# Backbone layer: when the weight sums of the fifth product are requested, who forms one sum, and who copies one head's output

## The chip, the cores and the metric

The kernel runs on one core of one Trainium2 chip. The metric is the device time of one execution in microseconds (us); lower is better. The kernel before was timed in 3 runs: median 903.42 us, from 902.72 to 903.51. One more execution was taken with the hardware profiler. It took 907.04 us, and all rows below come from it. Its span, from the first instruction to the last, is 905.3 us.

TensorE (PE) multiplies, VectorE (DVE) and ScalarE (ACT) do elementwise work, GpSimd (POOL) and SyncE (SP) mostly issue DMA transfers. Every transfer runs on the core's 16 DMA engines, whichever queue it was issued from. In the profile q0 is POOL's queue, q1 is SP's and q10 is ScalarE's.

## The reference

One layer of a diffusion backbone over 512 latent tokens and 256 context tokens, width 1024, all in float32. The part that matters here is the token mixer:

```python
z = h @ w_in
u, vs, q, r, ga, gb, k, v, lr = _split(z, IN_SPLITS)
a = _spatial_gating(gelu(u), gelu(vs), ...)
o, s_f, s_b = _gla_bidir(qh, k, v, lr, ...)          # 4 heads, chunked linear attention
o = o * lax.rsqrt(jnp.mean(o * o, axis=-1, keepdims=True) + EPS)
ob = (o * gla_norm_g) * jax.nn.silu(r)
merged = sigmoid(ga) * (a @ w_br_a) + sigmoid(gb) * (ob @ w_br_b)
return merged @ w_o
```

A modulated norm stands before it, and a convolutional feed-forward block with two more large products (`ffn_w_up`, `ffn_w_down`) behind it.

## The kernel before

**Arithmetic.** Every float32 operand of a product is split into a rounded high part and a remainder, and each product takes three matmuls (high by high, high by low, low by high). A weight tile goes from DRAM into a tile `raw` (SP issues it, L240), ScalarE rounds it to `wh` (the cast of L255), VectorE forms `wl = raw - wh` (L256), and PE uses the pair. `raw` has 5 buffers (`RAW`), `wh` and `wl` 5 each.

**Order of the work.** The weight tiles stand in one list, `specs`. A call of `weights()` takes the next pair; on the way it splits up to two tiles further (`stream_split`) and requests loads up to four tiles further (`stream_load`). Positions 0 to 17 serve the heads' q, k and v and then the eight column blocks of u (`u0` to `u7`, positions 10 to 17); `R_AT` is 18. Then come five large products of 14 positions each: r (18 to 31), vs (32 to 45), ga (46 to 59), gb (60 to 73) and the product with `w_br_a`, called br_a here (74 to 87). `w_br_b`, `w_o` and the feed-forward weights follow. In time r starts at 246.16 us, vs2 at 300.84, ga3 at 352.72 and gb at 378.1.

**The five products.** Each is done as a 2 by 2 block product with seven block products instead of eight (`gate`). Block product m of r is called r0 to r6, and so on; each takes two positions (two halves of the contraction) and 24 matmuls. Results lie in three pairs of PSUM banks, X, Z and Y, and go out by ScalarE copies (`taken`, L1341) or VectorE operations; bank pair X serves block products 0, 2, 4 and 6. The seven weight operands are three plain quarters of the weights and four sums of quarters.

**The sums.** Sums of quarters are formed in DRAM by transfers that POOL issues (`sums_build`): a plain copy of a quarter into a buffer `sum` (L221), then transfers that add a second quarter or another sum onto it (L223). Each carries 512 KB. A product needs 8 such requests per half, 16 in all. For the first three products (`g < ADDED`, r, vs and ga) the first sum is formed on the core instead: the positions of block product 1 load the second quarter raw, VectorE adds the raw tile of two positions earlier onto it (L251) before the cast, and 6 requests per half remain, 12 in all. The raw tile of two positions earlier keeps its buffer until that addition.

**When the sums are requested.** `gate_sums` walks through the requests of r, vs, ga, gb and br_a in this order, 68 in all. `weights()` takes the next one or two of them at each position below `R_AT`, and above it at those that `gate_pace` names; `hook()`, which is called between pieces of other work (twice in each u block), takes one more. `behind_pe` makes each request wait for the last matmul written before it.

```python
def gate_pace(i):
    return i % 3 if i > 45 else i % 4 == 0
...
def hook():
    hooked[0] += 1
    if (hooked[0] % 2 or pos[2] >= 8) and pos[2] < R_AT:
        next(building[1][1], None)
```

Followed by hand, this gives 42 requests before u0, 22 in u0 to u7 (10 of gb, of which 2 plain, and 12 of br_a, of which 8 plain), and one each at r1, r3, r5 and vs0.

**Other transfers around it.** In u, SP also reads back pieces of the normed input (`fq<-fx`) for the sums of activations. In r to ga it reads columns of `w_ada` (`wa`), and ScalarE's queue writes intermediate results to DRAM (`kept`). At the start of gb, SP reads `a` back in 16 pieces (`aq<-kept`, L1501).

**Head outputs.** `step_o` forms four output tiles of a head in PSUM; VectorE copies each to SBUF (L1020), and ScalarE then squares and sums the same tile (L1022). Only after both is the bank free. The four heads run between the other products; the second head (`h == 1`) ends at about 172 us.

Of the kernel before, what the change touches and what calls it, by code (L numbers as in the profile page):

```python
# [38 lines left out]
SHSC = 6  # L39
WT = (1, 1)  # L40
RAW = 5
ADDED = 3


@with_exitstack
def backbone_kernel(
# [7 lines left out]
    V, A, G, T = nc.vector, nc.scalar, nc.gpsimd, nc.tensor  # L54
# [19 lines left out]
    def late(shape, dt=F32, s="l"):  # L74
        return lp.tile(shape, dt, tag="l", name=nm(s))
# [7 lines left out]
    def gl():  # L83
        return pg.tile([P, 512], F32, tag="gl", name=nm("gl"))
# [81 lines left out]
    R_AT = len(specs)  # L166
# [14 lines left out]
    def w_block(ap, kn=2, back=0):  # L181
        specs.append((ap.rearrange("(k p) c -> p k c", p=P), kn, 512, back))
# [9 lines left out]
    for g, (g_quarter, g_sums) in enumerate(gate_weights):  # L192
        for n, f in enumerate((lambda b: g_quarter(b, 0, 0),
                               lambda b: g_quarter(b, 0, 1) if g < ADDED else g_sums[b][0], lambda b: g_sums[b][1],
                               lambda b: g_quarter(b, 1, 0), lambda b: g_sums[b][3], lambda b: g_quarter(b, 1, 1),
                               lambda b: g_sums[b][2])):
            for b in range(2):
                w_block(f(b), back=2 if n == 1 and g < ADDED else 0)
    down_specs[R_AT:R_AT] = specs
# [13 lines left out]
    def sums_build(quarter, sums, added=False):  # L213
        for step in ((((1, (0, 0)), (2, (1, 0)), (3, (0, 1))), ((3, (1, 1)),), ((1, 3),), ((2, 1),)) if added else
                     (((0, (0, 1)), (1, (1, 1)), (2, (1, 0)), (3, (0, 1))), ((0, (0, 0)), (3, (1, 1))),
                      ((1, 0),), ((2, 1),))):
            for b in range(len(sums)):
                for dst, src in step:
                    ap = quarter(b, *src) if isinstance(src, tuple) else sums[b][src]
                    if len(step) > 2:  # L220
                        behind_pe(lambda: G.dma_start(sums[b][dst], ap), G)  # L221
                    else:
                        behind_pe(lambda: G.dma_start(sums[b][dst], ap, accum_op=ALU.add), G)  # L223
                    yield

    def gate_sums():
        for g, z in enumerate(gate_weights):
            yield from sums_build(*z, g < ADDED)

# [3 lines left out]
    pos = [0, 0, 0]  # L233
# [37 lines left out]
        return lambda: V.tensor_tensor(wl, raw, wh.bitcast(F32), op=ALU.subtract)  # L271

    def gate_pace(i):
        return i % 3 if i > 45 else i % 4 == 0

    def weights():
        i = pos[2]
        pos[2] += 1
        for at, steps_ in building:
            for _ in range((i >= at and (at > 1 or i < R_AT or gate_pace(i))) + (at <= i < DENSE)):  # L280
                next(steps_, None)
        stream_split(i + 2)
        stream_load(i + 1 + AHEAD)
        return splits.pop(i)
# [648 lines left out]
    def mm3(ps, a, b, start, stop):  # L933
        for z, (p_, q_) in enumerate(((a[0], b[0]), (a[0], b[1]), (a[1], b[0]))):
            T.matmul(ps, p_, q_, start=(start and z == 0), stop=(stop and z == 2))  # L935
# [75 lines left out]
    def step_o(h, part):  # L1011
        S_ = heads[h]
        for i in ((1, 2), (0, 3))[part]:
            po = gl()
            oc = po[:, :256]
            for d in range(2):
                mm3(oc, [z[:, i * P:(i + 1) * P] for z in S_["qs"][d]], S_["st"][d][i], d == 0, False)
            mm3(oc, [z[:, i * P:(i + 1) * P] for z in S_["pt"]], S_["v"][i],
                False, True)
            V.tensor_copy(S_["o"][i // 2][:, i % 2, :], oc)  # L1020
            junk = late([P, 256], BF16, s="junk")
            A.activation(junk, oc, AF.Square, accum_out=oss[:, h, i:i + 1])  # L1022
        if part == 1:
            S_.clear()
# [3 lines left out]
    hooked = [0]  # L1028

    def hook():  # L1030
        hooked[0] += 1
        if (hooked[0] % 2 or pos[2] >= 8) and pos[2] < R_AT:
            next(building[1][1], None)
        if hooks:
            f = hooks.pop(0)
            f[0](*f[1:])
# [4 lines left out]
    def ctx_k(h, part):  # L1041
        ps = mm()
        for k in range(KT):
            wh, wl = part(k)
            ah, al = hc[k]
            for i, (a, b) in enumerate(((wh, ah), (wh, al), (wl, ah))):
                T.matmul(ps[:, :LC], a, b, start=(k == 0 and i == 0), stop=(k == KT - 1 and i == 2))  # L1047
        kcs[h] = heap([P, LC], s="kc")
        A.copy(kcs[h], ps[:, :LC])
        hook()  # L1050
# [5 lines left out]
    def x_unit(store, h):  # L1056
        w = weights()
        ps = mm()
        prod_cm(ps, w, hx)
        store[h] = heap([P, S], s="kq")  # L1060
        if store is qxs:
            A.mul(store[h], ps, QS)
        else:
            V.tensor_copy(store[h], ps)
        hook()
        return lambda k: [z[:, k, :] for z in w]

    def v_units():

        ws = [weights() for _ in range(KT // 2)]  # L1070
        v = []
        for t in range(6):
            ps = mm()
            for k in range(KT):
                wide_step(ps, ws[k // 2], hx if t < 4 else hc, t % 4, k)
            v.append(split_act(ps, s="v", lo_pool=late if t < 3 else heap, hi_pool=late, eng=A.copy))
            for h in (2, 3):
                heads[h].setdefault("v", []).append([z[:, (h - 2) * 256:(h - 1) * 256] for z in v[t]])
            hook()
            hook()  # L1080

    def steps(h):
        if h + 1 < NH:
            rest = [(step_u, h, 0, 3), (step_z, h + 1), (lambda: None,)]
        else:
            rest = [(step_u, h, n, n + 1) for n in range(3)]
        return [(step_transpose, h), (step_scores, h), (step_s0, h)] + rest + [(step_o, h, 0), (step_o, h, 1)]
# [854 lines left out]
```

## Time and profile before

| what | value |
|---|---|
| median of the timed runs | 903.42 us (902.72 to 903.51) |
| profiled execution | 907.04 us |
| its span | 905.3 us |
| PE busy | 888.0 us (98%) |
| VectorE busy | 733.9 us (81%) |
| ScalarE busy | 481.4 us (53%) |
| q0 (POOL): moved, share of 16 engines | 61.04 MB, 31.0% |
| q1 (SP): moved, share of 16 engines | 140.53 MB, 48.6% |
| mean granted TensorE clock | 0.996 of full |

A share of the DMA engines is the time that packets took, over 16 engines and the stretch in question. Packets overlap a little, so a full stretch shows up to about 1.1. The groups of the profile name a line, an engine, an operation and tiles as output<-input; "idle before" is the time that the engine waited just before the instruction, with what released it. The time to landing of a transfer runs from its issue to its completion.

### The profile page before, as it was taken

To read this page: it belongs to the slowest core of one execution; us is meant where nothing else is said; L and a number is where in the kernel's file an instruction comes from. 1 tells how busy PE (TensorE), PEld (TensorE's weight loads), DVE (VectorE), ACT (ScalarE), POOL (GpSimd) and SP (SyncE) were. 2 spreads that over 40 slices of the span, in tenths; PEclk is the share of its full clock that TensorE was granted. 3 is DMA by queue.
4 is the path that set the end of the run, shared out by engine and by line. 5 is a ranking of instruction groups with operands and counts; after the bars stand their busy time and mean duration, and the time that the engine had idled before them with its cause. 6 is when DMAs were issued, how large, how long until landed. Compare 5 with 4: busy or idle time off the path is not lost.

```text
span 905.3 us, 12519 instructions
## 1 busy us (share of the span) xinstructions
PE 888.0 (98%) x4440; PEld 739.6 (82%) x4440; DVE 733.9 (81%) x1223; ACT 481.4 (53%) x795; POOL 96.6 (11%) x150
## 2 busy tenths in 40 slices
PE   7999999999999999999999999999999999999996
PEld 5778888888877888888888889888888888888885
DVE  6478687969739889769998658897899987896996
ACT  6356465757636765577432348433343334356663
POOL 1302222222200000000000010001111110000000
PEclk9999999999999999999999999999999999999999
DMA  9976999999999977778995961998998893356552
GB/s 298 360 242 171 247 280 212 195 289 247 315 269 280 342 243 259 261 240 274 368 364 165 292 179 47 280 303 180 189 219 178 176 193 98 92 167 207 173 180 99
DMA packets 160268, 207.66 MB, mean 229 GB/s; under 512 B 9625, under 2 KB 88805, under 8 KB 160205
## 3 DMA queue, kind: packets, MB, share of 16 engines
q1 hardware_dynamic: 132861, 140.53, 48.6%
q0 software_dynamic: 24352, 61.04, 31.0%
q10 hardware_dynamic: 2992, 5.28, 1.5%
q8 instruction: 35, 0.57, 0.2%
q14 instruction: 28, 0.23, 0.1%
HBM read 198.43 MB, written 67.11 MB: 293 GB/s over the span
## 4 chain that ended last, share of the span: by engine, by line
PE 90%; DMA 4%; DVE 2%; ACT 2%; issue 0%; SPq 0%; ACTq 0%
PE mm L399 32%; PE mm L1358 13%; PE mm L417 10%; PE gl L1839 10%; PE gl L1358 5%; PE gl L935 2%; PE mm L699 2%; DMA fq<-fx 2%; DMA raw<-in_w_in_dram 2%; PE mm L1839 2%; PE gl L699 1%; PE mm L1047 1%; PE mm L1097 1%; PE gl L417 1%; PE gl L608 1%; PE gl L970 1%
## 5 line engine op out<-in xcount | busy, mean ns | idle before, releaser
L255 ACT CAST wh<-raw 128x1024 fp32r<-128x1024 f32 x189 | 194.8, 1036 | 189.3 <-PE mm L399 89.0
L256 DVE TENSOR_TENSOR wl<-raw,wh 128x1024 fp32r<-128x1024 f32 x189 | 226.1, 1203 | 61.8 <-ACT wh L255 60.2
L399 PE MATMUL mm<-h2h,wh 128*128 128x512 f32 (+1 forms) x344 | 133.0, 387 | 0.0
L399 PE MATMUL mm<-h2l,wh 128*128 128x512 f32 (+1 forms) x344 | 133.0, 387 | 0.0
L399 PE MATMUL mm<-h2h,wl 128*128 128x512 f32 (+1 forms) x344 | 133.0, 387 | 0.0
L1691 DVE SCALAR_TENSOR_TENSOR cacc<-ca,ccol,cacc 128x441 f32<-128x441 f32 (+2 forms) x176 | 121.9, 695 | 4.4
L399 PEld LDWEIGHTS mm<-h2h,wh 128*128 128x128 f32 x344 | 64.6, 188 | 13.1
L399 PEld LDWEIGHTS mm<-h2h,wl 128*128 128x128 f32 x344 | 64.6, 188 | 13.1
L399 PEld LDWEIGHTS mm<-h2l,wh 128*128 128x128 f32 x344 | 64.6, 188 | 13.0
L1839 PE MATMUL gl<-wh,dah 128*128 128x512 f32 x132 | 51.3, 389 | 0.0
L1839 PE MATMUL gl<-wl,dah 128*128 128x512 f32 x132 | 51.3, 389 | 0.0
L1839 PE MATMUL gl<-wh,dal 128*128 128x512 f32 x132 | 51.3, 389 | 0.0
L221 POOL DMA_DIRECT2D sum<-in_ffn_w_down_dram x24 | 13.2, 554 | 310.2 <-PE mm L417 196.1
L1188 DVE SCALAR_TENSOR_TENSOR acc<-wa,cs,acc 128x512 f32<-128x512 f32 x64 | 46.3, 749 | 0.0
L1692 ACT ACTIVATE cacc<-cacc 128x512 f32<-128x512 f32 x22 | 13.9, 633 | 59.4 <-DVE cacc L1691 59.4
L1358 PE MATMUL mm<-wh,xs 128*128 128x512 f32 x128 | 42.4, 402 | 2.7 <-ACT dt L1341 2.7
L223 POOL DMA_DIRECT2D sum<-sum x32 | 27.8, 869 | 149.0 <-PE mm L399 54.9
L399 PE MATMUL mm<-hxh,wh 128*128 128x512 f32 x104 | 40.9, 393 | 0.0
L399 PE MATMUL mm<-hxl,wh 128*128 128x512 f32 x104 | 40.6, 391 | 0.0
L399 PE MATMUL mm<-hxh,wl 128*128 128x512 f32 x104 | 40.5, 390 | 0.0
L1358 PE MATMUL mm<-wh,hxh 128*128 128x512 f32 x96 | 37.7, 393 | 0.0
L1358 PE MATMUL mm<-wh,hxl 128*128 128x512 f32 x96 | 37.4, 390 | 0.0
(473 smaller groups left out, 2018.0 us busy)
## 6 DMA issues: line engine op xcount, KB each, us to landing
raw<-sum SPq DMA_DIRECT2D x54, 512.0 KB, 4.9
raw<-in_w_in_dram SPq DMA_DIRECT2D x50, 512.0 KB, 9.2
wa<-in_w_ada_dram SPq DMA_DIRECT2D x96, 256.0 KB, 5.3
raw<-in_ffn_w_up_dram SPq DMA_DIRECT2D x44, 512.0 KB, 5.9
sum<-in_w_in_dram POOLq DMA_DIRECT2D x36, 512.0 KB, 8.8
sum<-sum POOLq DMA_DIRECT2D x30, 512.0 KB, 7.9
sum<-in_ffn_w_down_dram POOLq DMA_DIRECT2D x30, 512.0 KB, 7.2
raw<-in_ffn_w_down_dram SPq DMA_DIRECT2D x15, 512.0 KB, 3.7
```

What stands on the lines that cost most here:

```text
L223: behind_pe(lambda: G.dma_start(sums[b][dst], ap, accum_op=ALU.add), G)
L255: A.copy(wh, raw)
L256: V.tensor_tensor(wl, raw, wh.bitcast(F32), op=ALU.subtract)
L399: T.matmul(ps, a[:, k, :], b[:, c0:c0 + n], start=(k == 0 and i == 0), stop=(k == KT - 1 and i == 2))
L417: T.matmul(ps, a[:, t * P:(t + 1) * P], b[:, k % 2, :], start=(k == 0 and i == 0), stop=(k == KT - 1 and i == 2))
L699: T.matmul(fps[i], a, b, start=(k == 0 and z == 0), stop=(k == KT - 1 and z == 2))
L935: T.matmul(ps, p_, q_, start=(start and z == 0), stop=(stop and z == 2))
L1188: behind_last(lambda: V.scalar_tensor_tensor(acc[i], coming.pop(0), cs[:, k, 0:1], acc[i], op0=ALU.mult, op1=ALU.add), V)
L1358: T.matmul(banks[t], a(kk, t), w[:, kk, :], start=(first and b == 0 and kk == 0 and i == 0), stop=(b == 1 and kk == 1 and i == 2), skip_gr ...
L1691: V.scalar_tensor_tensor(o, a_[:, r0 + dy:r1 + dy, c0 + dx:c1 + dx], wcol(tap), o, op0=ALU.mult, op1=ALU.add)
L1692: A.activation(acc, acc, AF.Gelu)
L1839: T.matmul(ps, a, w[:, kk, :], start=(first and kk == 0 and i == 0), stop=(last and kk == n_ - 1 and i == 2), skip_group_check=True)
```

## The change

Three edits. First, gb joins the products whose first sum VectorE forms from two raw tiles (`ADDED` 4): gb has 12 requests instead of 16, in all 64 instead of 68, and VectorE has two more additions of 128x1024. Second, `hook()` takes no request once position 10 has been passed, so that in u only the eight `weights()` calls take one each; and `gate_pace` takes one at every fourth position in r and at every second from vs on. Followed by hand, u now has the last 6 requests of gb (all additions, u0 to u5) and 2 of br_a (u6, u7); r0, r2, r4 and r6 have one each, vs0 to vs6 one each, ga0 to ga2 one each. Of br_a's 16, the eight plain copies come from u6 to vs1, and the eight additions from vs2 to ga2. Third, the four output copies of the second head go from VectorE to ScalarE.

```diff
-ADDED = 3
+ADDED = 4
...
     def gate_pace(i):
-        return i % 3 if i > 45 else i % 4 == 0
+        return (i - R_AT) % (4 if i < R_AT + 14 else 2) == 1
...
-            V.tensor_copy(S_["o"][i // 2][:, i % 2, :], oc)
+            (A.copy if h == 1 else V.tensor_copy)(S_["o"][i // 2][:, i % 2, :], oc)
...
     def hook():
         hooked[0] += 1
-        if (hooked[0] % 2 or pos[2] >= 8) and pos[2] < R_AT:
+        if (hooked[0] % 2 or pos[2] >= 8) and pos[2] <= R_AT - 8:
             next(building[1][1], None)
```

## The prediction

> **What bounds the kernel now.** I read the head of the page first, then PE's waits, then the place of the longest wait that lies inside the work, engine by engine.
>
> ```profile
> span 905.3 us, 12519 instructions
> PE 888.0 (98%) x4440; PEld 739.6 (82%) x4440; DVE 733.9 (81%) x1223; ACT 481.4 (53%) x795; POOL 96.6 (11%) x150
> ...
> PE mm L463 <- DMA rows<-in_b_ada_dram: 5.5, 1, 5.5
> PE mm L1358 <- ACT dt L1341: 2.7, 1, 2.7
> ...
> 270.41 0.39 PE L1358 MATMUL mm<-wh,xs 128*128 128x512 f32 x1
> 273.53 0.80 PE L1358 MATMUL mm<-wh,xs 128*128 128x512 f32 x1 [2.73 <-ACT dt L1341]
> ...
> 276.54 0.39 PE L1358 MATMUL mm<-wl,xs 128*128 128x512 f32 x1
> ...
> 277.86 5.46 PE gl L1358 x24
> ...
> 270.00:275.00 5.00, 2.27 (x8) 1.52 (x7) 2.17 (x5) 3.06 (x7) 0.00 (x0) 0.80 0.89 315
> ```
>
> PE is the bound: 905.3 - 888.0 leaves 17.3 us, most of it at the two ends (5.5 us is the first load). No edit removes a matmul, so only a gap in PE's row can be won. In the middle there is one of size: in r4, 2.73 us, waiting for a bank that ScalarE had not copied out. It costs more than it shows. From 273.53 to 276.54 PE started 7 matmuls in 3.01 us; at the undisturbed pitch (5.46 / 24 = 0.2275) they need 1.59. The granted clock, column eight of the last row, is 0.80 of full over those 5 us. So 1.42 us went to the slow clock, and the gap is worth 2.73 + 1.42 = 4.15 us.
>
> The Trainium skill, "TensorE: Matmul & The Clock Gate", section "What's actually happening", has the clock halved after an idle window of about 3.4 us, by which a gap of 2.73 us could pass unpunished and removing it would be worth 2.73; the row with 0.80 shows the loss here, and I go by the row.
>
> Why was ScalarE late?
>
> ```profile
> 262.95 1.05 ACT L255 CAST wh<-raw 128x1024 fp32r<-128x1024 f32 x1 [5.12 <-DMA raw<-sum]
> 263.91 0.58 ACT L1341 COPY dt<-mm 128x512 f32<-128x512 f32 x1
> 266.69 1.05 ACT L255 CAST wh<-raw 128x1024 fp32r<-128x1024 f32 x1 [2.20 <-DMA raw<-sum]
> 271.94 1.04 ACT L255 CAST wh<-raw 128x1024 fp32r<-128x1024 f32 x1 [4.21 <-DMA raw<-in_w_in_dram]
> 272.89 0.58 ACT L1341 COPY dt<-mm 128x512 f32<-128x512 f32 x1
> ...
> 239.18 17.21 DMA fq<-fx
> 256.45 15.39 DMA raw<-in_w_in_dram
> ...
> q0 software_dynamic: 1064, 2.11, 76.0%
> q1 hardware_dynamic: 1067, 1.47, 33.0%
> ...
> 246.16:270.80 24.64, 24.64 (x109) 20.08 (x107) 10.96 (x12) 11.47 (x16) 2.63 (x3) 1.00 1.10 265
> ```
>
> ScalarE works in order. Three casts wait for weights (5.12, 2.20, 4.21 us), and the copy that PE needs stands behind the third. The chain that ended last agrees: a load of 15.39 us, behind one of 17.21. The two queue rows (245 to 260 us) say why. POOL's sums hold 76.0% of the DMA engines, SP's loads get 33.0%, and the last row shows 1.10 (column nine) for r0 to r4: the engines are full. Those sums are for gb and br_a, which need them more than 100 us later.
>
> **The change part by part.**
>
> *Fewer sums in u.* The gap goes if the loads land sooner. What one 512 KB sum costs, I take from the first two rows below: a stretch with q0 nearly alone (140 to 160 us, copies and additions mixed) and one with additions only (680 to 720 us). The next two rows are for 186 to 246 us, that is u; then come the first and the last of four additions in POOL's row, and POOL's next transfer after the gates.
>
> ```profile
> q0 software_dynamic: 1630, 4.38, 99.1%
> ...
> q0 software_dynamic: 1708, 3.27, 55.4%
> ...
> q0 software_dynamic: 3962, 10.57, 71.9%
> q1 hardware_dynamic: 5343, 6.26, 33.2%
> ...
> 239.49 0.90 POOL L223 DMA_DIRECT2D sum<-in_w_br_a_dram  x1 [5.05 <-DMA sum<-in_w_br_a_dram]
> ...
> 252.06 0.88 POOL L223 DMA_DIRECT2D sum<-sum  x1 [3.53 <-PE mm L1358]
> ...
> 466.50 0.59 POOL L221 DMA_DIRECT2D sum<-in_ffn_w_down_dram  x1 [176.57 <-PE mm L417]
> ```
>
> 0.991 x 20 us / 4.38 MB x 0.524 MB = 2.37 us of all 16 engines for the mix; 0.554 x 40 / 3.27 x 0.524 = 3.55 us for an addition. U had 22 requests and keeps 8. At 2.37 the 14 that leave are 33 us of full engines, in a stretch of 60 us that was full throughout (71.9 + 33.2 = 105.1%). That is several times the backlog that r inherits: a load that took 15.39 us made PE wait 2.73, so any landing under about 12.7 us is in time. Four new requests in r, all plain copies, are at most 4 x 2.37 = 9.5 us of DMA in 38 us, where the four additions issued from 239.49 to 252.06 us alone held 14.2 at 3.55. I take the whole gap as gone: -4.15 us in the profiled execution. Bounds: 0, if reading `fq` back and not the sums makes the loads late, and 4.15.
>
> *The four requests that vanish* (two copies, two additions) are part of that. POOL's queue holds nothing else that the requests are moved past (it idled for 176.57 us before 466.50), and the last sum, asked for at ga2, about 345 us, is for br_a, which begins at 417: nobody waits for it. VectorE takes over two additions:
>
> ```profile
> L251 DVE TENSOR_TENSOR raw<-raw,raw 128x1024 f32<-128x1024 f32 x6 | 7.3, 1212 | 1.3 <-DMA raw<-in_w_in_dram 1.3
> ...
> 378.10:417.20 39.10, 39.10 (x173) 32.24 (x173) 27.72 (x34) 29.45 (x43) 0.00 (x0) 1.00 0.77 246
> ...
> 376.14 8.49 SPq L1501 DMA_DIRECT2D aq<-kept  x16
> ...
> 390.62 1.05 ACT L255 CAST wh<-raw 128x1024 fp32r<-128x1024 f32 x1 [0.48 <-DMA raw<-sum]
> ```
>
> Two by 1.21 us on an engine that is busy 27.72 of 39.10 us in gb: nothing, with PE as cover; 2.4 us if VectorE were last there. The raw tiles of gb0 are held until the addition, about one block product (5.4 us) longer, so two loads are issued that much later, and the 16 reads of `aq` stand near them in SP's queue. The cast at 390.62 already waits 0.48 us for its load. But it serves gb4, the fourth block product after 378.1 us, about ten us later; the same hold in vs and ga left no PE gap. I take 0; bounds 0 and one gap of r4's kind, 4.15.
>
> *The second head's copies.*
>
> ```profile
> 167.53 2.00 ACT L255 CAST wh<-raw 128x1024 fp32r<-128x1024 f32 x2
> 170.50 0.38 ACT L1022 ACTIVATE junk<-gl 128x256 bf16<-128x256 f32 x1 [0.97 <-DVE o L1020]
> 169.98 1.42 DVE L1020 COPY o<-gl 128x256 f32<-128x256 f32 x4
> 171.03 1.21 PE L953 MATMUL gl<-ident,lx 128*128 128x128 f32 x6 [0.45 <-ACT junk L1022]
> 176.46 0.37 ACT L1049 COPY kc<-mm 128x256 f32<-128x256 f32 x1
> ```
>
> PE waits 0.45 us for a bank, because ScalarE's squares wait 0.97 for VectorE's copies. A 128x256 copy out of PSUM takes ScalarE 0.37. It is free at 167.53 + 2.00 = 169.53, so the first bank is done at 169.53 + 0.37 + 0.38 = 170.28 and not 170.88; later banks gain less, since each now takes both operations on one engine. I take -0.3; bounds +0.3 (the last banks come later) and -0.8 (ScalarE puts the copies before the casts). VectorE is 1.42 us freer; PE waits for it nowhere near.
>
> *The moved additions.* Eight additions of br_a now fall in vs2 to ga2, one in each block product. Below, the first row is from the feed-forward stage, the others from vs2 to ga2; column nine of the second is the DMA share.
>
> ```profile
> 563.54 184.99 PE mm L399 x816
> ...
> 300.84:352.72 51.88, 51.88 (x262) 43.59 (x261) 46.64 (x71) 35.87 (x48) 0.00 (x0) 1.00 0.81 270
> ...
> raw<-in_w_in_dram SPq DMA_DIRECT2D x9, 512.0 KB, 5.1
> ...
> 336.31 6.13 SPq L240 DMA_DIRECT2D raw<-sum  x2
> ...
> 344.35 1.04 ACT L255 CAST wh<-raw 128x1024 fp32r<-128x1024 f32 x1
> ```
>
> The stretch has no POOL transfer now, and a DMA share of 0.81: 0.81 x 51.88 = 42.0 us of work. A full stretch does 1.10, or 57.1. Eight additions bring 8 x 2.37 = 19.0 to 8 x 3.55 = 28.4. So at the end loads are behind by 42.0 + 19.0 - 57.1 = 3.9 us, or by 13.3. A load there lands in 5.1 us and could take 12.7 by r's measure: 7.6 are hidden. The middle, 8.6, is about what is hidden, and some of the 42.0 us was loads catching up after r's jam. I take 0; bounds 0 and the rival below.
>
> *The sum.* -4.15 - 0.3 = -4.45: the profiled execution would go from 907.04 to 902.59. It lies 3.62 us above the median, though, in a kernel whose PE work is the same every time. If nothing of the 3.62 is the gap, the median falls to 903.42 - 4.45 = 898.97. If all of it is the gap, the timed runs hold only 0.53 of it and fall to 902.59. Neither end is shown; I take the middle, 900.8.
>
> **The rivals.**
>
> *Slower: the gates starve.* The additions fill the DMA engines in vs2 to ga2 for long enough that the loads' lead is used up. The point: lateness over what is hidden. For: with 3.55 us per addition the loads are 13.3 us behind; and the lead in ga may be shorter than r's, since the load issued at 336.31 serves the cast at 344.35, and 8.0 less 5.1 leaves 2.9 us before ScalarE waits. ScalarE's wait of 4.21 made PE wait 2.73, so 1.5 more are hidden, 4.4 in all. Then PE loses 13.3 - 4.4 = 8.9 us, and 1.42 in each of at least two gaps: 11.7. Less 4.45, that is 910.7 at most. At the middle (8.6 behind) it is 8.6 - 4.4 + 1.42 - 4.45: +1.2 us, 904.6. So it is slower by over 0.2% from some 9.2 us behind. Against: in the feed-forward stage one addition every 5.4 us stood beside the loads, and PE kept 184.99 / 816 = 0.227 us per matmul, though it loads half as much per matmul there.
> The Trainium skill, "DMA: Bandwidth & Descriptors", section "Queues, rings and completion order", has each DMA engine take turns between queues packet by packet; by that even a single addition in flight slows every load beside it, which speaks against moving them here, and q0's 76.0% beside q1's 33.0% agrees with it.
>
> *No change: the gap is the profile's.* The timed runs hardly have it, and what is left is -0.3 for the head and about -0.5: 902.6. For: 3.62 is close to 4.15. Against: nothing says that profiling lengthens this place and not the start.
>
> *One gap comes back*, in ga or gb, of r4's size: 903.42 - 4.45 + 4.15 = 903.1. The same time follows if the edit doesn't do what it says, because the six additions of gb left in u (21 us at 3.55) and `fq` keep the loads late.
>
> **How the numbers follow.** This kernel's measurement can tell about 0.2%, 1.8 us, from no change: faster is below 901.6, slower above 905.2. The forecast, gap gone and nothing new with the gap at least half real in the timed runs, 0.50. The gap mostly the profile's, 0.18. One gap back or the jam left, 0.16: with the former both are same. The gates starve, 0.16: slower. So faster 0.50, same 0.34, slower 0.16. Point 900.8. The range reaches from 898.5 (the full gap, the head at -0.8) to 904.9, which takes in the cases without effect and the starving at its middle, and leaves out its upper half and little below. The likeliest case's own range is 898.5 to 901.6.
>
> **What would show it.** In the profile after: no PE wait for L1341 near 270 us and a granted clock of 1.00 through r; q0's share from 245 to 260 us down from 76.0% to some 10 to 20%; raw loads landing in under 8 us there; 8 additions at L251 and 12 copies at L1020 on VectorE; no PE wait for L1022 at 171 us; in vs2 to ga2 a DMA share of 1.0 to 1.1, and casts that wait for `raw` by under 3 us each. I am wrong if PE waits in vs, ga or gb by more than 1 us, or if the gap in r stays. If the profiled span falls by about 4 us and the median by less than 1, the gap was the profile's own.

## The result and the profile after

| | before | after |
|---|---|---|
| median of the timed runs | 903.43 us (13 runs, 902.72 to 905.85) | 909.40 us (13 runs, 902.86 to 912.27) |
| profiled execution, its span | 907.04, 905.3 us | 909.80, 908.1 us |

The ratio is 1.0051 [1.0032, 1.007]: the changed kernel is slower by 0.5%. That is the rival "the gates starve", not the forecast. Its times scatter over 9.4 us; those of before scatter over 3.1 here, but over 6.7 to 9.6 us in the 35 runs on each of the three chips used below. Two executions at a granted clock of 0.737 and 0.266 (1136.0 and 3258.61 us) are left out of all ratios and ranges. The page's head and PE's waits (line, what it waited for, us in total, times, longest):

```profile
span 908.1 us, 12503 instructions
...
PE 888.7 (98%) x4440; PEld 741.2 (82%) x4440; DVE 735.2 (81%) x1221; ACT 483.0 (53%) x799; POOL 94.2 (10%) x146
```

```profile
PE mm L463 <- DMA rows<-in_b_ada_dram: 5.9, 1, 5.9
PE gl L1227 <- ACT obf L1336: 5.0, 1, 5.0
```

The wait for L1341 in r and the wait for L1022 at 171 us are gone. A longer one has come, for a bank that ScalarE's `obf` (L1336) empties. First the edits that did what was forecast. These are the groups of lines, then the transfers between 245 and 260 us (per queue: packets, MB, share of the DMA engines; per load: count, KB each, us to landing), then r0 to r4 (start:end, length, busy time of PE, PEld, DVE, ACT and POOL, clock, DMA share, GB/s):

```profile
L251 DVE TENSOR_TENSOR raw<-raw,raw 128x1024 f32<-128x1024 f32 x8 | 9.7, 1213 | 0.0
L1020 DVE COPY o<-gl 128x256 f32<-128x256 f32 x12 | 4.6, 419 | 0.6 <-PE gl L935 0.6
```

```profile
q1 hardware_dynamic: 1371, 2.61, 57.0%
q0 software_dynamic: 202, 0.75, 19.6%
...
raw<-in_w_in_dram SPq DMA_DIRECT2D x2, 512.0 KB, 4.8
```

```profile
246.40:271.00 24.60, 24.60 (x111) 20.36 (x110) 16.91 (x23) 18.26 (x27) 1.67 (x3) 1.00 0.80 236
```

q0 holds 19.6% instead of 76.0%, raw loads land in 4.8 us instead of 15.39, and the stage's DMA share is 0.80 instead of 1.10. PE has no gap in r. Now vs2 to ga3, first as a whole and then the two stretches of 5 us around the new gap:

```profile
296.26:355.47 59.21, 54.19 (x261) 45.26 (x261) 45.60 (x69) 34.85 (x46) 7.31 (x8) 0.94 1.06 310
340.00:345.00 5.00, 0.23 (x1) 0.00 (x0) 2.52 (x4) 1.91 (x3) 0.00 (x0) 0.77 1.06 361
345.00:350.00 5.00, 4.74 (x16) 4.18 (x17) 2.63 (x4) 1.14 (x2) 0.87 (x1) 0.55 0.91 311
```

The same work that took 51.88 us takes 59.21: 7.33 more, 5.03 of them the gap and the other 2.30 the slow clock (0.55 of full behind it). The spans add up so:

| stretch | before | after | difference |
|---|---|---|---|
| start to r | 246.16 | 246.26 | +0.10 (in it: first load 0.4 later, head 0.45 less) |
| r to vs2 | 54.68 | 50.00 | -4.68 |
| vs2 to ga3 | 51.88 | 59.21 | +7.33 |
| ga3 to the end | 552.58 | 552.63 | +0.05 |
| span | 905.3 | 908.1 | +2.80 |

Why the gap? From 296 to 354 us the transfers, ScalarE's row, PE's row and the chain that ended last show it:

```profile
q1 hardware_dynamic: 5819, 11.08, 53.3%
q0 software_dynamic: 2194, 4.24, 41.5%
...
raw<-sum SPq DMA_DIRECT2D x8, 512.0 KB, 12.7
```

```profile
337.14 1.05 ACT L255 CAST wh<-raw 128x1024 fp32r<-128x1024 f32 x1 [2.77 <-DMA raw<-sum]
...
338.81 1.05 ACT L255 CAST wh<-raw 128x1024 fp32r<-128x1024 f32 x1
343.09 1.04 ACT L255 CAST wh<-raw 128x1024 fp32r<-128x1024 f32 x1 [3.23 <-DMA raw<-in_w_in_dram]
344.04 0.58 ACT L1341 COPY dt<-gl 128x512 f32<-128x512 f32 x1
344.51 0.69 ACT L1336 ACTIVATE obf<-gl,vec_b 128x512 f32<-128x512 f32 x1
```

```profile
345.26 2.07 PE L1227 MATMUL gl<-swT,dc 128*128 128x128 f32 x8 [5.03 <-ACT obf L1336]
```

```profile
328.02 1.14 DVE raw L251
329.16 1.13 DVE stats L1430 x2
330.29 12.72 DMA raw<-in_w_in_dram
...
343.09 1.04 ACT wh L255
344.13 0.29 ACT dt L1341
...
344.51 0.70 ACT obf L1336
...
345.26 2.07 PE gl L1227 x8
```

It is r4's picture two products later: a load lands late, a cast waits for it, and the bank's copy stands behind the cast. From the cast's start to PE's is 345.26 - 343.09 = 2.17 us. PE was ready at 345.26 - 5.03 = 340.23, so the cast had to begin by 338.06. The load was issued at 330.29: it could have taken 7.77 us and took 12.72. The difference, 4.95, is the gap to within 0.1 by construction, because the limit was worked back from the gap; what the rows add is how long this load could have taken.

The load needs a free raw tile. One came free at 328.02 + 1.14 = 329.16, when VectorE's addition (L251) of the block product ga1 ended. In the four other executions with this gap the load went out within 0.02 us of that point. Here it went out 1.13 us later; SP's queue shows a wait of 1.8 us for a `wa` transfer there, and why it waited stays open.

### The profile page after: what moved, and what is told of

Its sections match the earlier page's. It is cut to its first block, busy times and chain, and to the rows that moved or that the text cites. A ratio compares the mean times of both kernels' runs of the same rounds, so it can differ in the third digit from the quotient of the medians.

```text
span 908.1 us, 12503 instructions
## 1 busy us (share of the span) xinstructions
PE 888.7 (98%) x4440; PEld 741.2 (82%) x4440; DVE 735.2 (81%) x1221; ACT 483.0 (53%) x799; POOL 94.2 (10%) x146
## 4 chain that ended last, share of the span: by engine, by line
PE 93%; DVE 2%; DMA 2%; ACT 2%; issue 0%; ACTq 0%
PE mm L399 33%; PE mm L1358 14%; PE mm L417 11%; PE gl L1839 10%; PE gl L1358 5%; PE gl L935 3%; PE mm L699 2%; PE mm L1839 2%; DMA raw<-in_w_in_dram 1%; PE gl L699 1%; PE mm L1047 1%; PE mm L1097 1%; PE gl L417 1%; PE gl L608 1%; PE gl L1227 1%; PE gl L970 1%
```

## The experiments

The theory: eight additions at 3 us of all engines each fill the DMA engines in vs2 to ga2, loads land in 12.7 us instead of 4.4, and the lead does not cover that. Its rivals: VectorE's fourth sum, which holds raw tiles in gb, or the bare number and bytes of the requests issued there. The runs of the kernel before on the three chips used had medians of 904.29, 904.81 and 904.69 us (35 each); ratios are to the runs of the same chip.

**One edit alone.** The kernel before with `ADDED = 4`:

> The kernel before with the first edit alone: gb's first sum by VectorE, 64 requests, the old times of asking. Theory S (the additions of br_a moved into vs2 to ga2 starve the loads): this edit is innocent; two copies and two additions less in u, so 903.4 or up to 1.5 us less, no PE wait over 1 us in vs, ga or gb. Theory H (the raw tiles that are held until VectorE's addition delay the loads): a PE gap in gb, and most of the 6 us of the whole change: 906 to 909.

Measured 904.75, ratio 1.0006 [0.9993, 1.0018], profiled 904.11. VectorE's two additions cost nothing that can be seen, and gb has no gap, so the tiles held in gb are not the cause. In this one profile r has no gap over 0.8 us either, though q0 still holds 66.4% from 245 to 260 us.

The kernel before with the new times of asking alone:

```diff
-        return i % 3 if i > 45 else i % 4 == 0
+        return (i - R_AT) % (4 if i < R_AT + 14 else 2) == 1
...
-        if (hooked[0] % 2 or pos[2] >= 8) and pos[2] < R_AT:
+        if (hooked[0] % 2 or pos[2] >= 8) and pos[2] <= R_AT - 8:
```

> The kernel before with the new times of asking alone: 68 requests, of which those of br_a now fall from u7 to ga6. Theory S: as slow as the whole change or slower, since the additions go on to ga6 at one in each block product: 908 to 912, a PE gap of 3 us or more in ga, raw loads in vs and ga landing in 9 to 13 us. Theory H: no more than 904.5.

Measured 906.38, ratio 1.0013 [0.9995, 1.0031]: less than expected, and not separated from 1. The profiled execution (909.66) shows the gap itself, in the same place:

```profile
PE gl L1227 <- ACT obf L1336: 3.1, 1, 3.1
PE mm L417 <- DVE sga L1545: 1.1, 1, 1.1
```

The kernel before with the second head's copies alone:

```diff
-            V.tensor_copy(S_["o"][i // 2][:, i % 2, :], oc)
+            (A.copy if h == 1 else V.tensor_copy)(S_["o"][i // 2][:, i % 2, :], oc)
```

> The kernel before with the second head's four copies on ScalarE alone. Both theories: no part in the loss; 903.1 (0 to 0.5 us less than before), the PE wait of 0.45 us for L1022 at 171 us gone. A third theory, that ScalarE as the later engine delays what follows in the third head, gives 904 to 906.

Measured 904.37, ratio 1.0014 [0.9998, 1.003]; profiled 907.79, with the gap in r (3.4 us). PE's wait at 171 us is gone: PE is busy for all 20.00 us from 160 to 180 (19.44 before). Some 0.3 us of 900 is below what timed runs can tell.

The two small edits together, without the new times of asking:

> The whole change without the new times of asking (first and third edit). Theory S: within 1.5 us of before, on either side. A theory that the two edits add up to a loss together: 905.5 or more, 1.5 to 2 us over before.

Measured 904.06, ratio 0.9988 [0.997, 1.0006], profiled 904.99. Without the new times of asking nothing is lost. With them alone the gap is there in the profile, but the loss in the medians (906.38 against 904.29) is not clear of noise.

**The whole change once more.** The changed kernel itself, beside the kernels that follow:

> The whole change once more, on the chip of the next three. Theory S (the additions of br_a in vs2 to ga2 starve the loads): 906 to 911, scattered over 5 us or more, a PE gap of 3 us or more at ga2.

Measured 907.89 (904.59 to 913.6), ratio 1.0037 [1.0016, 1.0057]. The gap at L1227 was 2.8 us in this execution, just under the 3 expected, with the casts of the same loads waiting 1.69, 0.22 and 2.01 us. So the gap is real, and its size changes from run to run.

**Price or number?** The changed kernel, with the transfers of br_a that add onto `sum` issued as plain copies of the same 512 KB at the same times. This kernel leaves the second terms out of br_a's sums:

```diff
+    def sums_build(quarter, sums, added=False, adds=True):
...
-                        behind_pe(lambda: G.dma_start(sums[b][dst], ap, accum_op=ALU.add), G)
+                        behind_pe(lambda: G.dma_start(sums[b][dst], ap, **(dict(accum_op=ALU.add) if adds else {})), G)
...
-            yield from sums_build(*z, g < ADDED)
+            yield from sums_build(*z, g < ADDED, g < ADDED)
```

> The whole change, but br_a's eight additions are plain copies over the buffer (so br_a's weight sums, and the output, are left without the second terms). The same number of transfers at the same times, each at about half the price (4096-byte packets instead of two reads and a write). Theory S: no PE gap over 1 us in vs or ga, raw loads there landing in 6 to 9 us instead of 12.7, 901 to 903.5. Theory N (the number of requests or their order in POOL's queue matters, or the schedule that the compiler derives from them): as slow as the whole change, 906 to 911.

Measured 903.55, ratio 0.9983 [0.9967, 0.9998], profiled 903.33. Its stretch from 300 to 352 us as a window, then its transfers there:

```profile
300.00:352.00 52.00, 52.00 (x262) 43.70 (x261) 45.18 (x70) 33.18 (x44) 4.07 (x7) 1.00 0.97 332
```

```profile
q0 software_dynamic: 1152, 4.19, 24.7%
...
raw<-sum SPq DMA_DIRECT2D x7, 512.0 KB, 6.1
```

And the changed kernel in the same stretch:

```profile
q0 software_dynamic: 2086, 4.04, 43.9%
...
raw<-sum SPq DMA_DIRECT2D x5, 512.0 KB, 12.7
```

The same number of transfers and nearly the same bytes (4.19 and 4.04 MB), and no gap: PE is busy for all 52.00 us. A copy holds 0.247 x 52 / 4.19 x 0.524 = 1.61 us of all 16 engines, an addition 0.439 x 52 / 4.04 x 0.524 = 2.96. The requests and their bytes are not enough; the engines' time that adding takes on top of a copy is what the stretch lacks. Adding also brings more packets (2086 against 1152), and no run separates the two.

**Half as many there.** The changed kernel with one request at every fourth position throughout:

```diff
-        return (i - R_AT) % (4 if i < R_AT + 14 else 2) == 1
+        return (i - R_AT) % 4 == 1
```

> The whole change, but a request at every fourth position from r to the end of gb, so that the additions come one in two block products and reach into gb. Theory S: loads keep their lead, since an addition of about 3 us stands against two block products of about 12 us; no PE gap over 1 us in vs and ga, 901 to 903.5, and the scatter of the timed runs shrinks to about 2 us. Theory H: as slow as the whole change, 907 to 911.

Measured 906.28, ratio 1.0024 [1.0012, 1.0035]: a miss. Between 300 and 352 us there are now three additions and a copy instead of seven additions (22.4%, sums land in 8.9 us). The gap there shrinks to 1.0 us but does not vanish: the load that the chain goes through took 9.75 us and could take 8.88. And there is a second loss: the last requests now come at 380 to 404 us, in gb, and PE waits once more in br_a. PE's waits, then two windows of this kernel, then one of the level kernel that follows below:

```profile
PE gl L1227 <- ACT obf L1336: 1.0, 1, 1.0
PE mm L417 <- DVE sga L1545: 0.9, 1, 0.9
```

```profile
378.00:417.00 39.00, 38.91 (x171) 31.53 (x170) 28.28 (x35) 29.00 (x44) 2.62 (x3) 1.00 0.97 293
445.00:460.00 15.00, 14.05 (x62) 11.28 (x61) 15.00 (x21) 8.00 (x11) 0.00 (x0) 1.00 1.05 397
```

```profile
378.00:417.00 39.00, 39.00 (x173) 32.18 (x172) 30.67 (x39) 30.35 (x47) 0.00 (x0) 1.00 0.85 272
```

In br_a PE waits for VectorE, which is busy for all 15.00 us from 445 to 460; no late load stops it there. It comes in behind: in gb it did 28.28 us of work, and 30.67 in the level kernel. There a cast (at 390.02) waited 3.11 us for its load, and VectorE 7.79 us for the cast; in the level kernel the same two waits are 0.58 and 5.25. The DMA share of gb is 0.97 here and 0.85 there. So a late load in gb is paid for in br_a, where VectorE has no slack to catch up.

**Level.** The changed kernel with one request at every fourth position and eight more requests taken in u (16 instead of 8), so that neither u nor ga carries most of br_a:

```diff
-        return (i - R_AT) % (4 if i < R_AT + 14 else 2) == 1
+        return (i - R_AT) % 4 == 1
...
-        if (hooked[0] % 2 or pos[2] >= 8) and pos[2] <= R_AT - 8:
+        if (hooked[0] % 2 or pos[2] >= 8) and pos[2] <= R_AT - 4:
```

> The whole change, but hook() still takes requests up to position 14 (u0 to u3) and the rest come at every fourth position from r on, so that 16 are asked for in u, four in r and two in vs. Theory S: neither u and r nor vs and ga are full (DMA share in 300 to 352 us about 0.9), no PE gap over 1 us from r to gb, 900.5 to 903: the only version that should beat before. If what matters is instead the total of the work in u to ga, it is no better than before: 903.5 to 904.5.

Measured 902.51 (901.72 to 903.96), ratio 0.9975 [0.9963, 0.9987]; profiled 902.69, span 901.0. PE never waits over 0.4 us after the start. The stretch from 300 to 352 us:

```profile
300.00:352.00 52.00, 52.00 (x262) 43.71 (x261) 45.58 (x69) 33.34 (x43) 0.88 (x1) 1.00 0.85 276
```

The same kernel on another chip:

> The levelled times of asking once more: 902 to 903 and 0.15 to 0.35% under before; no PE gap over 1 us after the first load.

Measured 902.61, ratio 0.9972 [0.9956, 0.9987]. It beats both kernels, and with less scatter. The same with `ADDED = 3`, the sum of gb formed by transfers again:

> The levelled times of asking with the first sum of gb by transfers as before (68 requests, so four of br_a's additions follow in vs and ga at one in two block products). Theory S: two additions more in vs and ga than the levelled kernel and two in u, so between the two, 902.5 to 904; a gap of at most 1 us. If VectorE's sum is itself of use or of harm, it shows as over 1 us against the levelled kernel.

Measured 902.41, ratio 0.9962 [0.9947, 0.9977]. VectorE's sum shows no effect on the time.

**A longer lead.** The changed kernel with the same additions, and six raw tiles instead of five. `LATE = 25` takes one buffer from a pool of other tiles to make the room; it also runs alone.

```diff
-LATE = 26
+LATE = 25
...
-RAW = 5
+RAW = 6
```

> The whole change with six raw buffers instead of five, and one buffer less in the pool of late tiles to make room (LATE 25). Each load can be asked for one tile earlier, 2.7 us. Theory S (full DMA engines in vs2 to ga2 use up the loads' lead): the gap at ga2 falls by up to 2.7 us, and the median by 1.5 to 4 us against the next kernel. If the lead does not matter (the DMA engines are short by the same amount whatever the lead), no difference to the next kernel within 1 us.

> Control for the six raw buffers: the whole change with LATE 25 and five raw buffers. As slow as the whole change, 906 to 911, if one late tile less costs nothing; more if it does.

With six tiles 903.62, ratio 0.9986 [0.9964, 1.0008]; with `LATE = 25` alone 906.04, ratio 1.0013 [0.9989, 1.0038]. Six tiles under the same load of the DMA engines, as a window and in the landing of the sums:

```profile
300.00:352.00 52.00, 52.00 (x261) 43.48 (x260) 45.11 (x69) 33.32 (x44) 6.34 (x7) 1.00 1.08 317
```

```profile
raw<-sum SPq DMA_DIRECT2D x6, 512.0 KB, 12.2
```

The sums land in 12.2 us, the share is 1.08, and PE does not wait there. The load that made the gap lands about 10.0 us after its issue (330.12 to the cast at 340.20), longer than the 9.72 us that cost 0.7 us of gap with `LATE = 25` alone; with a sixth tile it goes out some 1.1 us earlier, set against PE's work. That is in line with the lead as the thing that decides. But the 2.4 us between the two medians are not separated, and with `LATE = 25` alone the gap was only 0.7 us in the one execution profiled, so this pair supports and does not prove.

All of it in one table, for 300 to 352 us (the before kernel has no addition there). "Load took" is the second load of ga3, through which the chain goes wherever there is a gap, from issue to landing; in the kernels with five raw tiles and no gap, its cast began 8.2 us after the issue without waiting for it. "Could take" is worked back from the gap, as above.

| kernel | q0's share | DMA share | sums land in, us (median) | load took, us | could take, us | gap at L1227, us | ratio |
|---|---|---|---|---|---|---|---|
| before | 0 | 0.82 | 4.4 | at most 8.2 | | 0 | 1 |
| level | 5.8% | 0.85 | 4.1 | at most 8.2 | | 0 | 0.9975 |
| half as many | 22.4% | 0.93 | 8.9 | 9.75 | 8.88 | 1.0 | 1.0024 |
| level, `ADDED = 3` | 24.8% | 0.97 | 6.6 | at most 8.2 | | 0 | 0.9962 |
| additions as copies | 24.7% | 0.97 | 6.1 | at most 8.2 | | 0 | 0.9983 |
| times of asking alone | 36.0% | 1.02 | 12.2 | 11.85 | 8.87 | 3.1 | 1.0013 |
| changed | 43.9% | 1.06 | 12.7 | 12.72 | 7.77 | 5.0 | 1.0051 |
| changed, again | 44.1% | 1.07 | 12.0 | 11.62 | 8.87 | 2.8 | 1.0037 |
| changed, `LATE = 25` | 44.1% | 1.08 | 11.4 | 9.72 | 9.06 | 0.7 | 1.0013 |
| changed, six raw tiles | 43.1% | 1.08 | 12.2 | about 10.0 | | 0 | 0.9986 |

With five raw tiles this load could take 8.87 to 9.06 us in four executions and 7.77 in the one where it went out late. Each kernel in which it came within 8.2 us has no gap. The stretch's share alone does not order the rows: "half as many" has 0.93 and a gap, "level, `ADDED = 3`" has 0.97 and none, with additions at nearly the same times (327.63 and 327.34 us beside this load). The additions read `w_br_a` in the first and `sum` in the second; whether that decides is not shown.

## Why the prediction was wrong

**The step that failed** is "the moved additions", which I took at 0 because "The middle, 8.6, is about what is hidden"; they measured +7.33 us in the profiled execution. The behind-hand side of that step was sound: 2.96 us per addition lies inside its bounds of 2.37 and 3.55, and the share of 1.06 inside the 1.0 to 1.1 that it named. With 2.96, the loads are 42.0 + 8 x 2.96 - 57.1 = 8.6 us behind, just the middle. The other side was not. "A load there lands in 5.1 us and could take 12.7 by r's measure: 7.6 are hidden": 12.7 was r's lead. Here the load had 7.77 us, and 8.87 to 9.06 in the other executions, so 2.7 to 4.0 were hidden beyond 5.1. By the prediction's own sum, 8.6 less that leaves a gap of 4.6 to 5.9 us; the two executions of the changed kernel had 5.03 and 2.83. What sets the lead here is a raw tile that VectorE's addition in ga1 holds (the load goes out as that addition ends), and not the pace of the list; the run with a sixth tile fits this. The rows of before already showed it: the load issued at 336.31 and its cast at 344.35, from which the rival worked out 4.4. I had both numbers and took the borrowed one. Two of the prediction's own signs came out against it: a cast in this stretch waited 3.23 us (it named under 3) and PE waited 5.03 (it named 1).

The Trainium skill, "DMA: Bandwidth & Descriptors", section "Queues, rings and completion order", says that each DMA engine takes turns between queues packet by packet. By that an addition in flight would slow the loads beside it, and it does: loads landed in 12.7 us beside additions and in 4.4 without. That fits the rule but does not show the turns themselves, and with a single addition (the level kernel) the median was 4.1.

**The rival's sum** had the right mechanism and place. Its 904.6 at the middle was 4.8 us short of 909.40. At 8.6 us behind it gave 8.6 - 4.4 + 1.42 = 5.6 us, and 7.33 were lost: 5.03 of gap (it had 4.2) and 2.30 of clock (it had 1.42, the price after a gap of 2.73). The timed median rose by 6.0 us, above the 2.8 of the profiled pair. Part of that is that the profiled execution of before, at 907.04, carries its own gap, which the timed runs of before hold only in part; the rival took the whole 4.45 off their median.

**The gap in r** went as forecast: -4.68 from r to vs2 against -4.15, q0's share 19.6% within "some 10 to 20%", landing 4.8 within "under 8". All ten profiled executions with the new or the level times of asking are without that gap. Of the four with the old times, two have it (2.7 and 3.4 us) and two have no wait over 0.8 us there; the latter two both have `ADDED = 4`, so whether that edit or chance removed it there is open.

**The head's copies**: PE's wait of 0.45 is gone, against 0.3 forecast. **The sum of gb and the vanished requests**: 0, as taken.

**The middle for the timed runs**: a kernel without gaps was to reach 900.8 on the scale of 903.42, a ratio of 0.9971. The level kernel, with all three edits at other times of asking and no gap, has 0.9975 and 0.9972. That agrees, but as ratios to runs of before at 904.81 and 904.69 and not 903.42, so luck may have part in it. The forecast is about what such edits give when the additions do not starve ga. How much of r's gap the timed runs of before hold stays open: no trace of them exists. Their scatter on the three chips (902.35 to 909.09, 902.72 to 910.36, 902.27 to 911.83), beside 901.72 to 903.96 for the level kernel, fits a gap that comes and goes, but that is argued and not shown.

**The chance**: 0.16 for the starving gates was too low. It rested on the feed-forward stage, where additions stood beside loads at no cost, though it "loads half as much per matmul". That row could not speak for a stage whose DMA share was 0.81 before the additions came.

## What to carry to other kernels

Work that leaves a full stretch must be priced where it lands: that stretch's own DMA share, plus the engine time of the transfers that come. Measure how late a load may be in that place, from its issue to the last moment at which the chain behind it does not stop the bounding engine, and do not borrow that lead from another stage. Where every stretch is near full, spread the transfers evenly: the level kernel differs from the changed one only in the times of asking, and takes 0.25% less than before where that one takes 0.4 to 0.5% more.

## What the runs showed of the hardware that was not expected

- A transfer that adds onto DRAM held the 16 DMA engines for 2.96 us per 512 KB between 300 and 352 us, a plain copy in its place for 1.61.
- The clock's price is not in proportion to the gap: 1.42 us after a gap of 2.73, 2.30 after 5.03 (clock 0.55 over the next 5 us), and none that shows after 1.0 (half as many requests: clock 1.00 from 300 to 345 and from 345 to 380 us). After gaps of 2.83 and 3.05 us the clock was 0.70 and 0.74 from 345 to 350 us (changed kernel again, times of asking alone).
- Scatter goes with a gap that comes and goes: the changed kernel's 13 runs span 9.4 us, before's span 6.7 to 9.6 on the later chips, the level kernel's 2.2 and 1.5. It is a hint and no more, since the kernel with copies has no gap in its profile and spans 4.3.
